# Reordering the first projections of an encoder block: high-part products first, a second load queue, the norm's row first, weight conversions later

## The chip, the cores and the metric

The kernel runs on one core of one Trainium2 chip. The metric is the device time of one execution, in microseconds (us). The times of before are the median and the ends of three runs. The profile is of one further execution, and it has a time of its own.

## The reference

One encoder block on 1024 tokens of width 1024, to which 16 meta tokens are added (1040 in all), in float32:

```python
h = concatenate([meta, x])
proj = rms_norm(h, norm_mix) @ w_in          # 4352 columns: qa ka va qb kb vb and two gates
y_a = differential_attention(qa, ka, va)     # 4 heads, all keys
y_b = windowed_gqa(qb, kb, vb, sink)         # 8 heads on 2 key heads, window 128 and the meta tokens
h = h + (sigmoid(ga) * (y_a @ w_ba) + sigmoid(gb) * (y_b @ w_bb)) @ w_o
h = h + (silu(rms_norm(h) @ w_gate) * (rms_norm(h) @ w_up)) @ w_down
out = rms_norm(h, norm_final)[16:]
```

The change lies in the first microseconds: the norm of the first tokens, and the projections to kb and to the first two 128-column parts of qb.

## The kernel before, in words

**Products in three terms.** A float32 operand is held as a high part (rounded to fp32r by ScalarE, line 113 for weights, 146 for tokens) and a low part (what the rounding left, a subtraction at line 114 on POOL or VectorE for weights, 147 on VectorE for tokens). A product is then three matmuls: high by high, high weights by low tokens, low weights by high tokens. `project_steps` (line 201) does a projection of 128 columns: for each chunk of tokens and each of eight 128-row slices c of the weights it issues the three matmuls (line 208) into one PSUM bank, and yields after each slice. When the last slice is done, `evac_split` (lines 221 to 232) takes the bank out, again in a high and a low part, and `kb_consume` or `qb_steps` stores it.

**The first tokens.** Tokens come in tiles of 128. `load_x` (373) loads one, `norm_x` (380) normalises it: ScalarE squares and sums (130), POOL makes the reciprocal root (118, 119), VectorE multiplies by it and by the norm's row `gmix` (136). `turn_x` (387) transposes it on TensorE, four 128x128 blocks to a bank, two banks (144), and takes the banks out into `hT_hi` (146) and `hT_lo` (147). A chunk of kb or qb has 256 tokens, so its matmuls need two tiles turned. `gmix` is loaded as 32 rows and copied twice by VectorE to 128 (409 to 411).

**The weights.** `preload` (172) loads 128 columns of `w_in`; `ensure` (194) loads if needed and converts the next in a fixed order: kb's low part is made on POOL, qb's on VectorE. A third set, `w_q1` (second part of qb), has a tile of its own, shares its buffers with the token tiles, and is split at line 426 with VectorE.

**Keeping TensorE busy.** Fifteen matmuls on zeros (406) at the start and seven more (424), which wait for the first normalised tile, do no part of the result.

**What sets the order.** The kernel's text is written once in program order, but the tile framework schedules this part: it simulates the engines and emits each engine's instructions in the order of that simulation. Each engine then runs its own list in order, waiting at semaphores. DMAs are issued by SP's list, and one DMA waits in that list for all that stand ahead of it. `early` and `advance` (391) interleave the projections with the turning of later tiles. From the differential attention on, the order of the instructions is written out by hand.

The list of SP before begins: token tile 0 (line 376), `gmix` (409), token tile 1, kb's weights, qb's weights (174), `w_q1` (415), token tile 2, two small rows, token tile 3, and so on. Token tile 3 takes the buffer of tile 0, tile 4 that of tile 1, tile 5 that of `w_q1`.

ScalarE's list before: square of tile 0, square of tile 1, kb's conversion, the two takings-out of turned tile 0, qb's conversion, `w_q1`'s conversion, the two takings-out of tile 1, squares of tiles 2 and 3.

VectorE's list before: copies of `gmix`, norm of tile 0, the zeros, norm of tile 1, low parts of tile 0, low parts of qb's weights and of `w_q1`, two small rows (486, 490), low parts of tile 1, norms of tiles 2 and 3.

## Time and profile before

| what | us |
|---|---|
| median of 3 runs | 1447.68 (1447.35 to 1448.65) |
| the profiled execution's own time | 1447.04 |
| its span, first to last instruction | 1445.1 |
| TensorE busy in the span | 1429.7 (99%) |
| VectorE, ScalarE, POOL busy | 901.6, 675.1, 465.3 |

The views give a start in us from the span's start, then the busy time, the engine (PE is TensorE's matmuls, PEld its weight loads, DVE VectorE, ACT ScalarE, SPq and ACTq the DMA-issuing lists of SP and ScalarE), the line in the kernel, the operation, and what it writes and reads. A merged row has a count behind it. Square brackets tell how long the engine was idle ahead of the row and what ended that. The share of TensorE's clock that was granted is the column PEclk.

### The profile page before, as it was taken

To read this page: it belongs to the slowest core of one execution; us is meant where nothing else is said; L and a number is where in the kernel's file an instruction comes from. 1 tells how busy PE (TensorE), PEld (TensorE's weight loads), DVE (VectorE), ACT (ScalarE), POOL (GpSimd) and SP (SyncE) were. 2 spreads that over 40 slices of the span, in tenths; PEclk is the share of its full clock that TensorE was granted. 3 is DMA by queue.
4 is the path that set the end of the run, shared out by engine and by line. 5 is a ranking of instruction groups with operands and counts; after the bars stand their busy time and mean duration, and the time that the engine had idled before them with its cause. 6 is when DMAs were issued, how large, how long until landed. Compare 5 with 4: busy or idle time off the path is not lost.

```text
span 1445.1 us, 20977 instructions
## 1 busy us (share of the span) xinstructions
PE 1429.7 (99%) x7327; PEld 1229.1 (85%) x7327; DVE 901.6 (62%) x1758; ACT 675.1 (47%) x1275; POOL 465.3 (32%) x454
## 2 busy tenths in 40 slices
PE   8999999999999999999999999999999999999998
PEld 6989989888899999888878888888888888888886
DVE  7356426537777778635988875654455443777566
ACT  6355426534554546445345754333333333444444
POOL 4142223322323232221513135454445442000442
PEclk9999999999999999999999999999999999999999
DMA  7334353354424242079341633433223322964343
GB/s 229 87 99 115 108 128 92 89 174 133 139 82 140 89 140 82 22 241 298 117 160 64 191 110 110 146 125 108 97 97 108 102 102 98 342 207 140 125 124 146
DMA packets 159050, 191.67 MB, mean 133 GB/s; under 512 B 16113, under 2 KB 103601, under 8 KB 158945
## 3 DMA queue, kind: packets, MB, share of 16 engines
q1 hardware_dynamic: 158368, 189.28, 41.0%
q8 instruction: 58, 0.95, 0.3%
q10 hardware_dynamic: 576, 1.05, 0.2%
q14 instruction: 48, 0.39, 0.1%
HBM read 129.80 MB, written 53.94 MB: 127 GB/s over the span
## 4 chain that ended last, share of the span: by engine, by line
PE 94%; DVE 2%; DMA 2%; ACT 1%; issue 1%; POOL 0%; SPq 0%; DVEq 0%; ACTq 0%
PE pg L1233 29%; PE pd L1337 14%; PE pp_g L208 12%; PE aps L618 4%; PE po L1137 4%; PE apy L660 3%; PE pp_va L208 3%; PE pp_ka L208 3%; PE pp_qb L208 3%; PE pp_qa L208 3%; PE ppa L562 3%; PE apt L647 2%; PE bpt L346 2%; PE bpy L352 2%; PE bps L321 2%; PE po L1145 2%
## 5 line engine op out<-in xcount | busy, mean ns | idle before, releaser
L1233 PE MATMUL pg<-t,wop 128*128 128x512 f32 x1056 | 242.4, 389 | 0.0
L1233 PEld LDWEIGHTS pg<-t,wop 128*128 128x128 f32 x1056 | 198.3, 188 | 41.1
L1337 PE MATMUL pd<-ob,oa 128*128 128x512 f32 x924 | 209.6, 389 | 0.0
L114 POOL TENSOR_TENSOR wop<-wf,wop 128x512 fp32r<-128x512 f32 x114 | 151.3, 1327 | 164.2 <-ACT wop L113 155.7
L1337 PEld LDWEIGHTS pd<-ob,oa 128*128 128x128 f32 x924 | 173.5, 188 | 36.0
L1233 PE MATMUL pg<-b,wop 128*128 128x512 f32 x792 | 183.3, 390 | 0.4 <-ACT c L1245 0.4
L1233 PEld LDWEIGHTS pg<-b,wop 128*128 128x128 f32 x792 | 148.5, 188 | 31.3 <-ACT c L1245 0.7
L114 POOL TENSOR_TENSOR wl_c<-w_c,wh_c 128x1024 fp32r<-128x1024 f32 x32 | 78.2, 2443 | 154.3 <-ACT wh_c L113 132.6
L113 ACT ACTIVATE wop<-wf 128x512 fp32r<-128x512 f32 x128 | 80.8, 633 | 72.4 <-PE pg L1233 50.8
L629 ACT ACTIVATE as<-as,amn 128x1040 f32<-128x1040 f32 x64 | 74.5, 1165 | 73.6 <-DVE amn L624 73.6
L208 PE MATMUL pp_g<-hT_hi,wh_c 128*128 128x512 f32 x256 | 101.3, 396 | 0.0
L208 PE MATMUL pp_g<-hT_hi,wl_c 128*128 128x512 f32 x256 | 100.9, 394 | 0.0
L208 PE MATMUL pp_g<-hT_lo,wh_c 128*128 128x512 f32 x256 | 100.9, 394 | 0.0
L113 ACT ACTIVATE oa<-ra 128x512 fp32r<-128x512 f32 x77 | 48.7, 632 | 107.9 <-PE pd L1337 48.7
L618 PE MATMUL aps<-ak,aq 128*128 128x352 f32 (+1 forms) x384 | 92.6, 326 | 0.0
L114 POOL TENSOR_TENSOR oa<-ra,oa 128x512 fp32r<-128x512 f32 x27 | 34.9, 1294 | 168.6 <-ACT oa L113 167.2
L1011 DVE TENSOR_TENSOR s<-wf,wf 128x512 f32<-128x512 f32 x22 | 15.9, 724 | 110.0 <-DMA wf<-in_w_ff_up_dram 68.9
L618 PEld LDWEIGHTS aps<-ak,aq 128*128 128x128 f32 x384 | 69.6, 188 | 14.0
L624 DVE CUSTOM_DVE_ANT_0 as<-aps,dist,amn 128x352 f32<-128x352 f32 (+1 forms) x128 | 71.3, 563 | 10.4 <-PE aps L618 8.4
L333 POOL TENSOR_SCALAR bs<-bs,bdn 128x432 f32<-128x432 f32 (+1 forms) x64 | 37.0, 596 | 97.5 <-DVE bdn L331 56.2
L323 DVE CUSTOM_DVE_ANT_0 bs<-bps,tbx,nsink 128x432 f32<-128x432 f32 (+1 forms) x64 | 38.4, 624 | 41.1 <-PE bps L321 38.5
L624 DVE CUSTOM_DVE_ANT_0 as<-aps,dist,far_a 128x352 f32<-128x352 f32 x64 | 37.1, 580 | 43.0 <-PE aps L618 42.8
(276 smaller groups left out, 3049.7 us busy)
## 6 DMA issues: line engine op xcount, KB each, us to landing
ra<-aop SPq DMA_DIRECT2D x77, 256.0 KB, 2.6
w_c<-in_w_in_dram SPq DMA_DIRECT2D x33, 512.0 KB, 3.9
wf<-in_w_ff_gate_dram SPq DMA_DIRECT2D x25, 512.0 KB, 3.6
wf<-in_w_ff_up_dram SPq DMA_DIRECT2D x25, 512.0 KB, 3.6
aop<-as SPq DMA_DIRECT2D x44, 256.0 KB, 2.1
aop<-c SPq DMA_DIRECT2D x33, 256.0 KB, 2.0
g_d<-gate_stage SPq DMA_DIRECT2D x32, 256.0 KB, 2.0
gt<-g_d SPq DMA_DIRECT2D x32, 256.0 KB, 4.3
```

The lines of the kernel that those rows point to most:

```text
L113: nc.scalar.activation(hi, src, AF.Copy)
L114: lo_eng.tensor_tensor(lo, src, f32(hi), ALU.subtract)
L208: nc.tensor.matmul(ps[:, :n], a[:, c, :], b[:, c, at:at + n], start=(c == 0 and i == 0), stop=(c == DC - 1 and i == 2))
L323: nc.vector.tensor_tensor_reduce(st[:, r, :W], ps[:, :W], tb, 2.0 ** -(4 * g + r + 1), nsink[:, 4 * g + r:4 * g + r + 1], ALU.add, ALU.min ...
L562: nc.tensor.matmul(ps, w[:, a, j, :], src(j, b, tk), start=(j == 0 and n == 0), stop=(j == 3 and n == 2))
L618: nc.tensor.matmul(ps[:, :n], qs[m][:, t * P:(t + 1) * P], ks[m][:, vv, k0:k0 + n], start=(vv == 0), stop=(vv == 1))
L624: nc.vector.tensor_tensor_reduce(s[m][:, a:b], ps[:, a - k0:b - k0], far_by, slope, low, ALU.add, ALU.min, mn[:, m, i + j:i + j + 1])
L629: nc.scalar.activation(s[m][:, 0:L], s[m][:, 0:L], AF.Exp, bias=low, scale=-1.0, accum_out=dn[:, m:m + 1])
L660: nc.tensor.matmul(py[:, cols], v[:kp, a, k, :], at_[:kp, k, b, :], start=(k == 0 and j == 0), stop=(k == 8))
L1137: nc.tensor.matmul(sets_o[p][u], oa[:, a, u * P:(u + 1) * P], ob[:, b, :], start=(p in (1, 5) and j == 0 and k == 0), stop=(p in (2, 3) an ...
L1233: nc.tensor.matmul(ps, op[:, x, c, :], b[:, y, c, :], start=(p in (1, 5) and c == 0 and n == 0), stop=(p in (4, 2, 3) and c == 3 and n == ...
L1337: nc.tensor.matmul(ps[u], oa[:, a, u * P:(u + 1) * P], ob[:, b, :], start=(p in (1, 2, 5) and j == 0 and k == 0), stop=(p in (2, 3, 4) and ...
```

## The change

Five edits, all within the first stage:

1. **High parts first.** `project_steps` takes `hi_first`. With it, the first chunk (`at == 0`) issues its eight high-by-high matmuls first and then the sixteen others. It is set for kb and for the first two parts of qb. The number of matmuls and of yields is the same.
2. **Second tokens by ScalarE's queue.** Token tile 1 is issued from ScalarE's list (its first instruction, ahead of the load of the activation table) and no longer from SP's.
3. **The norm's row first.** `gmix` is now SP's first DMA, token tile 0 its second.
4. **Weights' conversions behind the tokens'.** The weights are loaded where they were, but kb's conversion is held back until the last high part of tile 0 is issued, and qb's and `w_q1`'s until that of tile 1 (`tc.issue_after`). The load of token tile 3 moves ahead of `w_q1`'s split in the program's text.
5. **Small rows later.** `gsub` and `nsink` (486, 490) wait for the last low part of token tile 3.

```diff
     def transposed(pp, xn, parts, hi, lo, at, name):
...
-            nc.scalar.activation(h, pt[:, :, :parts], AF.Copy)
-            nc.vector.tensor_tensor(lo[:, 4 * b:4 * b + 4, at:at + parts], pt[:, :, :parts], f32(h), ALU.subtract)
+            high = nc.scalar.activation(h, pt[:, :, :parts], AF.Copy)
+            low = nc.vector.tensor_tensor(lo[:, 4 * b:4 * b + 4, at:at + parts], pt[:, :, :parts], f32(h), ALU.subtract)
+        return high, low
...
-    def project_steps(col, chunks, name, evac):
+    def project_steps(col, chunks, name, evac, hi_first=False):
...
+            turns = [(c, i) for c in range(DC) for i in range(3)]
+            if hi_first and at == 0:
+                turns.sort(key=lambda ci: ci[1] > 0)
+            for u, (c, i) in enumerate(turns):
+                a, b = terms[i]
+                nc.tensor.matmul(ps[:, :n], a[:, c, :], b[:, c, at:at + n], start=(u == 0), stop=(u == 3 * DC - 1))
...
-    load_x(0)
     nc.sync.dma_start(gmix[0:32], norm_mix.broadcast_to([32, D]))
     nc.vector.tensor_copy(gmix[32:64], gmix[0:32])
     nc.vector.tensor_copy(gmix[64:P], gmix[0:64])
-    load_x(1)
-    ensure(2)
+    load_x(0)
+    load_x(1, nc.scalar)
+    preload(C_KB)
+    preload(C_QB)
...
-    turn_x(0)
+    high, _ = turn_x(0)
...
+    with tc.issue_after(high.ins):
+        ensure(1)
+    load_x(3)
+    high, _ = turn_x(1)
     q1_h, q1_l = (bpool.tile([P, DC, P], F32R, tag=tag, name=f"{tag}_q1", bufs=1) for tag in ("wh", "wl"))
-    split(q1_h, q1_l, w_q1, nc.vector)
+    with tc.issue_after(high.ins):
+        ensure(2)
+        split(q1_h, q1_l, w_q1, nc.vector)
     prepped[C_QB + P] = q1_h, q1_l
-    load_x(3)
     norm_x(2)
-    turn_x(1)
-    p_kb = project_steps(C_KB, KB_CHUNKS, "kb", evac_split(None, kb_consume))
+    p_kb = project_steps(C_KB, KB_CHUNKS, "kb", evac_split(None, kb_consume), hi_first=True)
...
-    nc.vector.tensor_scalar(gsub, gsub, 1.0 - LAMBDA_INIT, None, ALU.mult)
+    with tc.issue_after(low.ins):
+        nc.vector.tensor_scalar(gsub, gsub, 1.0 - LAMBDA_INIT, None, ALU.mult)
...
-    nc.vector.tensor_scalar(nsink, sinkb, -1.0, None, ALU.mult)
+    with tc.issue_after(low.ins):
+        nc.vector.tensor_scalar(nsink, sinkb, -1.0, None, ALU.mult)
```

What the scheduler makes of it: ScalarE's list now begins with the DMA of token tile 1, then squares of tiles 0 and 1, the two takings-out of tile 0, kb's conversion, the two of tile 1, qb's and `w_q1`'s conversions, squares of tiles 2, 3 and 4. VectorE's has the low parts of both tiles 0 and 1 ahead of those of qb's weights and `w_q1`. On TensorE the first products are eight high-by-high of kb, one with kb's low tokens, six high-by-high of qb, and only then those with kb's low weights; the whole first chunk (72 matmuls) stands nearly complete ahead of the turning of tiles 2, 3 and 4, which before were mixed into it. Up to the second group's projections of the windowed attention (about 180 us in the profile) the lists differ in places; then they are the same. The counts of all engines' instructions are the same, but for the one DMA that moved.

More of the change, by code (lines that the diff above doesn't have):

```diff
@@ L205, in project_steps @@
             ps = pp_bank(f"pp_{name}_{at}")
-            for c in range(DC):
-                for i, (a, b) in enumerate(terms):
-                    nc.tensor.matmul(ps[:, :n], a[:, c, :], b[:, c, at:at + n],
-                                     start=(c == 0 and i == 0), stop=(c == DC - 1 and i == 2))
-                if c == DC - 1:
+            turns = [(c, i) for c in range(DC) for i in range(3)]
[4 more added lines that the diff above has]
+                nc.tensor.matmul(ps[:, :n], a[:, c, :], b[:, c, at:at + n], start=(u == 0), stop=(u == 3 * DC - 1))
+                if u == 3 * DC - 1:
                     evac(ps[:, :n], at, n)
-                yield
+                if u % 3 == 2:
+                    yield
     def project(col, chunks, name, evac):
@@ L296, in consume @@
                                       st[64 * par:64 * par + 64, hl, :n])
-        return project_steps(C_QB + j * P, QB_CHUNKS if j < 2 else Q_CHUNKS, f"qb{j}", evac_split(qbs[:, j:j + 1], consume))
+        return project_steps(C_QB + j * P, QB_CHUNKS if j < 2 else Q_CHUNKS, f"qb{j}", evac_split(qbs[:, j:j + 1], consume),
+                             hi_first=j < 2)
     def project_qb(g, qb):
@@ L371, in encoder_block, with load_x @@
     xts, xns, done, early = {}, {}, [], []
-    def load_x(t):
+    def load_x(t, queue=nc.sync):
         xts[t] = bpool.tile([P, D], F32, tag="btr", name=f"x_{t}", bufs=4)
         if t < NT:
-            nc.sync.dma_start(xts[t], x[t * P:(t + 1) * P, :])
+            queue.dma_start(xts[t], x[t * P:(t + 1) * P, :])
         else:
@@ L388, in turn_x @@
         parts = P if t < NT else NM
-        transposed(lambda name: bank(psum1, ("bt", "bs")[t % 2], name, 2), xns.pop(t), parts, hT_hi, hT_lo, t * P, f"a{t}")
+        return transposed(lambda name: bank(psum1, ("bt", "bs")[t % 2], name, 2), xns.pop(t), parts, hT_hi, hT_lo, t * P, f"a{t}")
     def advance(n):
@@ L440, in encoder_block @@
     norm_x(4)
-    turn_x(3)
+    _, low = turn_x(3)
     early += [(p_kb, DC), (p_q0, DC), (p_q1, DC)]
```

## The prediction

> **What bounds the kernel now.** The page comes first, then the waits of TensorE (PE), then the first 25 us of the timeline.

> ```profile
> span 1445.1 us, 20977 instructions
> PE 1429.7 (99%) x7327; PEld 1229.1 (85%) x7327; DVE 901.6 (62%) x1758; ACT 675.1 (47%) x1275; POOL 465.3 (32%) x454
> ```

> ```profile
> PE pp_kb L208 <- DVE hT_lo L147: 2.1, 1, 2.1
> PE ptn_a L144 <- DVE xn_a L136: 1.7, 1, 1.7
> PE pp_kb L208 <- ACT hT_hi L146: 1.4, 1, 1.4
> PE idle L406 <- DVE zeros L403: 1.2, 1, 1.2
> PE po L1137 <- DVE gt L912: 1.1, 1, 1.1
> PE bps L321 <- DVE bmn L323: 1.0, 3, 0.4
> ```

> PE is the bound. Of its longest waits (total, count, longest in us) four lie in the first 16.5 us; the next is 1.1. So whatever brings PE's real work forward in the first stage should come out at the end one for one, and nothing else in this change can matter much. The profiled execution took 1447.04, 1.94 over its span, and lies 0.64 under the median of the three runs (1447.68).

> ```profile
> 0.72 0.40 SPq L376 DMA_DIRECT2D x<-in_x_dram  x1
> 1.17 0.42 SPq L409 DMA_DIRECT2D gmix<-in_norm_mix_dram  x1
> 1.17 5.99 PE L406 MATMUL idle<-zeros 128*128 128x512 bf16 x15 [1.17 <-DVE zeros L403]
> 4.95 1.06 ACT L130 ACTIVATE xn_a<-x 128x1024 f32<-128x1024 f32 x1 [2.95 <-DMA x<-in_x_dram]
> ...
> 7.49 1.28 DVE L136 SCALAR_TENSOR_TENSOR xn_a<-x,rstd_a,gmix 128x1024 f32<-128x1024 f32 x1 [0.72 <-POOL rstd_a L119]
> 7.63 1.06 ACT L130 ACTIVATE xn_a<-x 128x1024 f32<-128x1024 f32 x1 [1.53 <-DMA x<-in_x_dram]
> ...
> 8.83 1.09 PE L144 MATMUL ptn_a<-ident,xn_a 128*128 128x128 f32 x8 [1.67 <-DVE xn_a L136]
> ...
> 9.76 1.67 PE L424 MATMUL idle<-zeros 128*128 128x512 bf16 x7
> ...
> 10.26 3.22 POOL L114 TENSOR_TENSOR wl_c<-w_c,wh_c 128x1024 fp32r<-128x1024 f32 x1 [0.33 <-ACT wh_c L113]
> ...
> 12.20 1.06 ACT L113 ACTIVATE wh_q<-w_q 128x1024 fp32r<-128x1024 f32 x1
> 12.36 2.20 DVE L114 TENSOR_TENSOR wl_c<-w_c,wh_c 128x1024 fp32r<-128x1024 f32 x1
> 13.16 1.06 ACT L146 ACTIVATE hT_hi<-ptn_a 128x512 fp32r<-128x512 f32 x2
> 13.79 0.39 PE L208 MATMUL pp_kb<-hT_hi,wh_c 128*128 128x256 f32 x1 [1.41 <-ACT hT_hi L146]
> 14.14 0.28 PE L208 MATMUL pp_qb<-hT_hi,wh_q 128*128 128x256 f32 x1
> 14.48 1.21 DVE L114 TENSOR_TENSOR wl_q<-w_q,wh_q 128x1024 fp32r<-128x1024 f32 x1
> 15.75 1.28 DVE L147 TENSOR_TENSOR hT_lo<-ptn_a,hT_hi 128x512 fp32r<-128x512 f32 x2
> 16.48 0.44 PE L208 MATMUL pp_kb<-hT_lo,wh_c 128*128 128x256 f32 x1 [2.06 <-DVE hT_lo L147]
> 19.92 0.36 PE L208 MATMUL pp_qb<-hT_hi,wl_c 128*128 128x256 f32 x1
> ```

> The first product starts at 13.79. After three of them PE stops until 16.48, because VectorE (DVE) splits the weights of qb and `w_q1` (2.20 and 1.21) ahead of the low part of token tile 1. From 16.48 to 19.92 sixteen products start, 0.215 each. The rate afterwards is in one row of the chain (start, us, count): 0.118 each.

> ```profile
> 29.04 1.89 PE pp_kb L208 x16
> ```

> The windows of the span say why (stretch, length, busy time of PE, PEld, DVE, ACT and POOL, then the granted clock, the DMA share and GB/s):

> ```profile
> 16.00:17.00 1.00, 0.52 (x3) 0.52 (x4) 1.00 (x3) 0.40 (x2) 0.80 (x3) 0.83 0.88 266
> 17.00:18.00 1.00, 1.00 (x7) 1.00 (x6) 1.00 (x2) 0.00 (x0) 0.32 (x1) 0.50 0.85 280
> 20.00:22.00 2.00, 2.00 (x18) 2.00 (x18) 1.28 (x1) 0.00 (x0) 0.49 (x1) 0.98 1.11 411
> ```

> The clock halves at about 16.66 and returns at about 20.08, 3.4 us later. I measure the stage by an **effective start**: when the first chunk's 72 products would have to start to run without a gap at 0.118. Before, 19 products had started by 19.92: 19.92 - 19 x 0.118 = **17.7**.

> **The change part by part.**

> *Second queue and norm's row.* These decide the sum. Tile 0 is issued at 0.72 and landed by 4.95, when its square starts. The view of transfers gives the two behind it, from issue to landing:

> ```profile
> x<-in_x_dram SPq DMA_DIRECT2D x1, 512.0 KB, 6.0
> gmix<-in_norm_mix_dram SPq DMA_DIRECT2D x1, 128.0 KB, 4.2
> ```

> Tile 1 needs 6.0 (landed 7.63), behind all that was queued ahead. `gmix` (1.17 + 4.2 = 5.4) was not late: tile 0's norm waited for POOL until 7.49. Putting it first removes no wait and moves tile 0's issue 0.45 back. And tile 1, issued on ScalarE's list at the same moment, no longer waits behind tile 0. No row of the start has two queues loading; the end of the kernel has, when SP (q1) and ScalarE (q10) store together:

> ```profile
> q10 hardware_dynamic: 93, 0.19, 50.2%
> q1 hardware_dynamic: 95, 0.19, 49.8%
> ```

> Equal halves. So tile 0 (with `gmix` ahead, 640 KB) and tile 1 (512 KB) finish near together, near where tile 1 landed. Bounds for tile 0's landing: 5.4 (4.95 + 0.45, no sharing) and 7.63 (tile 1's row). I take 6.9, nearer the upper, a little under it because `gmix`'s two small shares now fall into the slow first microseconds. [...]

> From tile 0's landing to its transposes: 8.83 - 4.95 = 3.88, unchanged (square, POOL, norm). They start at 10.8, not 8.83. Tile 1's own norm is no longer late: its square follows tile 0's at once.

> *The clock.* PE's first idle products end at 7.16, so the gap is 3.6 us, not 1.67. A gap of 2.06 (with 0.6 of work and 1.41 of idling ahead of it) halved the clock, the 1.67 did not. I take it as halved at 10.8 and back 3.4 us of work later, at 14.2.

> *Stage by stage.* Eight transposes at half rate (twice 0.11 each): 12.6. Seven idle products: four at 0.40 (5.99 / 15, the half rate) until 14.2, three at 0.24 (1.67 / 7): 14.9. Tile 1's first four transposes, 0.55: 15.45; ScalarE's first taking-out, 0.53: 16.0, the second 16.55. Then eight high-by-high products of kb and one low: 9 x 0.118, 17.05. qb's conversion now stands behind both takings-out: 16.55 + 1.06 = 17.6; six high-by-high of qb, 18.3. kb's low weights: tile 0 taken out at 13.15, conversion 14.2, POOL 3.22, 17.45, in time. Fifteen products by 18.3 is an effective start of 18.3 - 15 x 0.118 = **16.55**, a gain of **1.15 us**.

> *High parts first* adds no matmul. It gives PE 14 products to do while POOL and DVE make low parts, which is what covers the 2.06 gap. *Conversions later* takes 3.4 us of DVE from ahead of `hT_lo` of tile 1, and two of ScalarE's 1.06 from ahead of its `hT_hi`. The price is that low weights are late next: qb's would be ready at 19.8 (17.6 + 2.20), and PE needs them after kb's other 15 products and eight more, at 21.0 (18.3 + 23 x 0.118). *Small rows later* frees at most 0.1 us of DVE (between the end of `w_q1`'s split, 15.69, and the low part's start, 15.75): nothing, as `hT_lo` is no longer last.

> *What is late behind it.* SP's list is in order; token tile 5 takes `w_q1`'s buffer, which is free only when DVE has split it (15.7 before, now about 19.9), and tile 3 waits for tile 0's norm (2 us later). Tile 5's square stands on ScalarE between the takings-out of tiles 2 and 3.

> ```profile
> 23.51 2.53 DVE L147 TENSOR_TENSOR hT_lo<-ptn_a,hT_hi 128x512 fp32r<-128x512 f32 x4 [0.35 <-ACT hT_hi L146]
> ```

> Before, tile 3's low part was done at 26.04 and its first use was at 29.04: 3 us of cover. Now the use comes at 16.55 + 72 x 0.118 + 24 transposes (2.7) = 27.75, and DVE gets there at 27.5 to 29; half of it is enough for the first 12 products. I cost it at nothing; without that cover it is up to 1 us. The mixed order of the windowed attention is worth between +1.0 and -1.0 (PE's only waits there, L321, are 1.0 in three); I take 0.

> Sum: 1447.04 - 1.15 = 1445.9, and for the median of runs 0.64 more: **1446.5**.

> **The rivals.**

> 1. *The clock holds across the 3.6 us gap.* Then transposes 10.8 to 11.7, idle products to 13.4, `hT_hi` of tile 1 at 14.4 and 14.95, qb's conversion 16.0, its six products 16.7; POOL's low weights 16.6. Effective start 16.7 - 1.77 = 14.95: 2.75 gained, 1444.9. For it: the 1.67 gap did no harm. Against: the 2.06 gap did. [...]
> 2. *No sharing at the start: tile 0 lands at 5.4.* Its transposes start at 9.3, the gap is 2.1, the clock holds. Idle products to 11.9, `hT_hi` of tile 1 at 12.9 and 13.45, conversion 14.5, six products 15.2: effective start 13.45, gain 4.25, 1443.4. Against: the equal halves of the tail.
> 3. *Slower: the half clock lasts through the stage.* Tile 0 lands at 7.63, transposes 11.5 to 13.25, seven idle products at 0.40 to 16.05, `hT_hi` of tile 1 at 17.5 and 18.0, conversion 19.1, six products at half rate 20.4: effective start 18.6, a loss of 0.9, 1448.6. It decides from the point where the clock returns after about 16.
> 4. *Tile 5 comes late and takes the gain.* Issued at 20, landing after up to 6.0 (tile 1's row), its square, from 26.0 and not from 25, holds up tile 3's taking-out and PE's second chunk by 0.9: gain 0.25, 1447.4. For it: the buffer is 4 us later. Against: less is queued ahead of it, so 4 is likelier.

> **How the numbers follow.** Forecast 0.45, rival 1 0.17, rival 2 0.12, rival 3 0.12, rival 4 0.14. 0.2% is 2.9 us (about what a measurement of this kernel can tell from no change), so "faster" is below 1444.8 and "slower" above 1450.6. Below lie rival 2 (0.12), nearly half of rival 1 (0.07) and the forecast's edge (0.05): 0.24. Above is only rival 3 with a second bad step: 0.04. Within: 0.72. The range takes in the forecast, rivals 1, 3 and 4, and rival 2 almost to its value: 1443.6 to 1448.8.

> **What would show it.** Right: ScalarE's first square starts at 6.5 to 7.5, PE's first transposes near 10.8, a PEclk under 1 somewhere between 9 and 15 and none at 16 to 20, the first product near 16.0, and after it no PE wait over 0.6 in the stage. A first square at 5.4 is rival 2; a first square at 7 with fast transposes is rival 1; a first product after 17 is rival 3; a PE wait near 28 is rival 4. What would make all of it wrong is a PE wait after 60 us that before did not have.

## The result and the profile after

| | before | after |
|---|---|---|
| median of the runs side by side, us | 1448.24 (1446.22 to 1451.5, 22 runs) | 1446.41 (1443.65 to 1448.74, 22 runs) |
| the profiled execution's own time | 1447.04 | 1446.66 |
| its span | 1445.1 | 1444.8 |

The ratio is 0.9985, with a 95% interval from 0.9979 to 0.9992: 1.83 us less, faster by less than the 0.2% that the prediction took as its bound. The forecast was 1446.5.

The page of after, its first rows:

```profile
span 1444.8 us, 20969 instructions
PE 1429.3 (99%) x7327; PEld 1227.7 (85%) x7327; DVE 904.0 (63%) x1758; ACT 674.4 (47%) x1275; POOL 470.2 (33%) x454
```

TensorE's waits in after (total, count, longest, in us):

```profile
PE ptn_a L145 <- DVE xn_a L136: 4.1, 1, 4.1
PE idle L413 <- DVE zeros L410: 1.2, 1, 1.2
PE po L1152 <- DVE gt L927: 1.2, 1, 1.2
PE apt L662 <- DVE as L650: 1.0, 1, 1.0
PE pg L1248 <- ACT c L1260: 0.9, 1, 0.9
PE bps L328 <- DVE bmn L330: 0.3, 1, 0.3
PE pp_kb L214 <- ACT hT_hi L147: 0.3, 1, 0.3
```

The waits of 2.1 and 1.4 ahead of kb's first products have shrunk to one of 0.3. In their place the wait for the first normalised tile is 4.1, not 1.7. The timeline of after, first 18 us (start, length, engine and line; the line numbers are those of the changed kernel, up to 15 above those of before):

```profile
6.75 1.06 ACT L130 ACTIVATE xn_a<-x 128x1024 f32<-128x1024 f32 x1 [4.30 <-DMA x<-in_x_dram]
7.80 1.04 ACT L130 ACTIVATE xn_a<-x 128x1024 f32<-128x1024 f32 x1
8.86 1.28 DVE L136 SCALAR_TENSOR_TENSOR xn_a<-x,rstd_a,gmix 128x1024 f32<-128x1024 f32 x1 [2.93 <-POOL rstd_a L119]
10.19 1.13 PE L145 MATMUL ptn_a<-ident,xn_a 128*128 128x128 f32 x8 [4.09 <-DVE xn_a L136]
11.05 1.28 DVE L136 SCALAR_TENSOR_TENSOR xn_a<-x,rstd_a,gmix 128x1024 f32<-128x1024 f32 x1 [0.45 <-POOL rstd_a L119]
11.12 3.19 PE L432 MATMUL idle<-zeros 128*128 128x512 bf16 x7
12.99 2.35 POOL L114 TENSOR_TENSOR wl_c<-w_c,wh_c 128x1024 fp32r<-128x1024 f32 x1 [1.98 <-ACT wh_c L113]
14.11 1.25 PE L145 MATMUL ptn_a<-ident,xn_a 128*128 128x128 f32 x8
15.58 1.29 DVE L148 TENSOR_TENSOR hT_lo<-ptn_a,hT_hi 128x512 fp32r<-128x512 f32 x2 [2.05 <-ACT hT_hi L147]
15.61 1.23 PE L214 MATMUL pp_kb<-hT_hi,wh_c 128*128 128x256 f32 x8 [0.25 <-ACT hT_hi L147]
17.85 0.28 PE L214 MATMUL pp_kb<-hT_hi,wl_c 128*128 128x256 f32 x1
```

Tile 0 is 1.80 later (6.75 against 4.95), its transposes 1.36, the first product 1.82 (15.61 against 13.79), but from there on nothing stops: fifteen products stand ahead of 17.85, so the effective start is 17.85 - 15 x 0.118 = 16.08, against 17.7. The windows of after (granted clock third from the end):

```profile
10.00:11.00 1.00, 0.81 (x7) 0.81 (x8) 0.56 (x2) 0.11 (x1) 0.92 (x2) 1.00 1.17 383
11.00:12.00 1.00, 1.00 (x6) 0.43 (x5) 0.95 (x1) 1.00 (x3) 0.01 (x1) 0.56 1.07 335
14.00:15.00 1.00, 1.00 (x8) 0.89 (x7) 0.00 (x0) 0.04 (x1) 1.00 (x1) 0.74 0.29 77
17.00:18.00 1.00, 0.95 (x8) 0.96 (x9) 0.97 (x1) 1.00 (x2) 0.00 (x0) 1.00 0.66 187
```

The 3.41 us of half clock that lay on the products from 16.66 now lies from 11.1 to 14.5 on the idle products and the first transposes of tile 1. How far the first stage as a whole has moved can be read from the first product of vb, behind kb and qb. The view of that tile, in before and then in after (count, ns least/median/most, first start to last):

```profile
L208 PE MATMUL pp_vb<-hT_hi,wh_c x24: 286/335/341, 58.2 to 69.8; 128*128 128x384 f32 x16, 128*128 128x272 f32 x8
```

```profile
L214 PE MATMUL pp_vb<-hT_hi,wh_c x24: 286/335/341, 56.9 to 68.5; 128*128 128x384 f32 x16, 128*128 128x272 f32 x8
```

The stage is **1.3 us** ahead. When the same matmul is compared by its number in the two traces, the lead is 1.32 at 57 us and 1.9 from 180 to 336 us: the waits of the windowed attention (L321, three with 1.0 in all; now L328, one of 0.3) give 0.6 more. Then this execution gives back 1.2 around `apt` (a wait of 1.0) and 0.5 at `pg` (0.9 against 0.4 in before). These two belong to the single execution: the changed kernel's second trace (below) has no `apt` wait and 0.5 at `pg`, and ends 1.93 ahead. So the medians' 1.83 agrees with the lead of 1.9, and the 0.38 between the two profiled executions does not contradict it.

### The profile page after: what moved, and what is told of

Read it like the earlier page. It is cut to its first block, busy times and chain, and to the rows that moved or that the text cites. A ratio compares the mean times of both kernels' runs of the same rounds, so it can differ in the third digit from the quotient of the medians.

```text
span 1444.8 us, 20969 instructions
## 1 busy us (share of the span) xinstructions
PE 1429.3 (99%) x7327; PEld 1227.7 (85%) x7327; DVE 904.0 (63%) x1758; ACT 674.4 (47%) x1275; POOL 470.2 (33%) x454
## 4 chain that ended last, share of the span: by engine, by line
PE 94%; DVE 3%; DMA 1%; ACT 1%; issue 1%; POOL 0%; SPq 0%; DVEq 0%; ACTq 0%
PE pg L1248 29%; PE pd L1352 14%; PE pp_g L214 12%; PE aps L633 4%; PE po L1152 4%; PE apy L675 3%; PE pp_va L214 3%; PE pp_ka L214 3%; PE pp_qb L214 3%; PE pp_qa L214 3%; PE ppa L577 3%; PE apt L662 2%; PE bpt L353 2%; PE bpy L359 2%; PE bps L328 2%; PE po L1160 2%
## 5 line engine op out<-in xcount | busy, mean ns | idle before, releaser
L114 POOL TENSOR_TENSOR wop<-wf,wop 128x512 fp32r<-128x512 f32 x114 | 154.2, 1354 | 162.5 <-ACT wop L113 150.7
L114 POOL TENSOR_TENSOR wl_c<-w_c,wh_c 128x1024 fp32r<-128x1024 f32 x32 | 77.3, 2416 | 170.2 <-ACT wh_c L113 160.0
L113 ACT ACTIVATE wop<-wf 128x512 fp32r<-128x512 f32 x128 | 80.7, 632 | 74.3 <-PE pg L1248 44.9
L113 ACT ACTIVATE oa<-ra 128x512 fp32r<-128x512 f32 x77 | 48.7, 632 | 108.3 <-PE pd L1352 50.1
L114 POOL TENSOR_TENSOR oa<-ra,oa 128x512 fp32r<-128x512 f32 x27 | 35.0, 1296 | 168.6 <-ACT oa L113 167.2
L1026 DVE TENSOR_TENSOR s<-wf,wf 128x512 f32<-128x512 f32 x22 | 15.2, 692 | 113.0 <-DMA wf<-in_w_ff_up_dram 61.5
L113 ACT ACTIVATE wh_c<-w_c 128x1024 fp32r<-128x1024 f32 x33 | 34.9, 1059 | 63.7 <-PE pp_g L214 28.1
L340 POOL TENSOR_SCALAR bs<-bs,bdn 128x432 f32<-128x432 f32 (+1 forms) x64 | 37.1, 599 | 82.3 <-DVE bdn L338 57.6
## 6 DMA issues: line engine op xcount, KB each, us to landing
w_c<-in_w_in_dram SPq DMA_DIRECT2D x33, 512.0 KB, 4.1
wf<-in_w_ff_gate_dram SPq DMA_DIRECT2D x25, 512.0 KB, 3.8
wf<-in_w_ff_up_dram SPq DMA_DIRECT2D x25, 512.0 KB, 3.8
```

What stands on the lines that cost most here:

```text
L113: nc.scalar.activation(hi, src, AF.Copy)
L114: lo_eng.tensor_tensor(lo, src, f32(hi), ALU.subtract)
```

## The experiments

**The theories.** The prediction's, A: loading tile 1 beside tile 0 delays tile 0, that halves the clock early, and the order of products together with the late conversions earns more than this costs. Against it: B1, the start is not what matters, since token tile 5, whose buffer comes free late, takes any gain; B2, the halved clock decides; B3, the order of products or the late conversions are worth nothing by themselves.

In the expectations of the single runs "theory A" and "theory B" are what stands there. Ratios are to before on the same chip, whose medians were 1447.77 (33 runs, first group), 1447.89 (30, second) and 1447.44 (26, third); after was measured beside 1448.24, as above. The ratios differ by up to 0.0006 from the quotients of the medians, so the two columns can put close kernels in a different order. "Square", "turn" and "product" are the starts of tile 0's square, of its transposes and of the first product; "vb" is the first product of vb (the stage's end), all in the one profiled execution. A lead is the time by which TensorE is ahead of before at the same number of matmuls; the time given with it is that of before up to 33 us.

| kernel | median | ratio, 95% interval | square | turn | product | vb |
|---|---|---|---|---|---|---|
| before | | 1 | 4.95 | 8.83 | 13.79 | 58.2 |
| after | 1446.41 | 0.9985 [0.9979, 0.9992] | 6.75 | 10.19 | 15.61 | 56.9 |
| again (1st) | 1446.08 | 0.9988 [0.9978, 0.9998] | 6.52 | 9.97 | 15.25 | 56.5 |
| x1_sp (1st) | 1444.88 | 0.9986 [0.9976, 0.9995] | 4.80 | 8.25 | 11.98 | 57.6 |
| x0_first (1st) | 1445.05 | 0.9983 [0.9975, 0.9992] | 5.10 | 9.03 | 12.95 | 59.1 |
| long_idle (1st) | 1446.34 | 0.9994 [0.9985, 1.0003] | 6.31 | 9.76 | 13.48 | 56.7 |
| tile5_early (2nd) | 1443.98 | 0.9971 [0.9960, 0.9982] | 4.87 | 8.32 | 12.05 | 53.5 |
| x0_tile5 (2nd) | 1444.88 | 0.9976 [0.9967, 0.9984] | 5.09 | 8.99 | 12.72 | 55.4 |
| conv_early (2nd) | 1445.54 | 0.9987 [0.9977, 0.9996] | 6.74 | 10.20 | 15.82 | 56.4 |
| no_hi (2nd) | 1447.4 | 0.9994 [0.9985, 1.0003] | 6.52 | 9.97 | 13.70 | 55.4 |
| queue_only (3rd) | 1449.6 | 1.0016 [1.0007, 1.0025] | 6.83 | 10.27 | 16.70 | 60.4 |
| after_t5 (3rd) | 1446.17 | 0.9988 [0.9980, 0.9997] | 6.57 | 10.02 | 16.52 | 58.0 |
| t5_again (3rd) | 1442.74 | 0.9970 [0.9958, 0.9981] | 5.45 | 8.89 | 12.62 | 53.9 |
| t5_no_hi (3rd) | 1443.36 | 0.9971 [0.9960, 0.9982] | 5.17 | 8.62 | 12.35 | 54.1 |

### again: the changed kernel once more

No edit.

> The changed kernel, unchanged. In the profile after, PE's work was 1.3 us ahead of before when the stage ended (57 us) and 1.9 ahead at 180 us, then lost 1.2 at a wait of 1.0 for VectorE near 340 us (L662) and 0.5 near 840 us. Theory (the waits belong to that one execution): neither wait comes back, and the median is 1.5 to 2 us under before. Rival (they belong to the changed order): the same two waits come back at the same places, and each costs 0.5 to 1.2 us in every run.

Tile 0's square is at 6.52, the gap ahead of the transposes 2.85, the half clock from 9.77 to 13.19, the stage 1.7 ahead (56.5 against 58.2). The windows of again, which show both ends of the half clock:

```profile
8.00:10.00 2.00, 0.03 (x1) 0.03 (x1) 1.33 (x2) 0.71 (x2) 1.73 (x2) 0.94 1.16 353
12.00:14.00 2.00, 2.00 (x8) 0.81 (x7) 1.31 (x3) 1.52 (x2) 0.40 (x1) 0.70 0.65 232
```

The late tile and an early half clock are in both traces; the wait at `apt` is not in this one, and that at `pg` is 0.5. Two traces of one kernel differ by 0.4 at the stage's end, so differences below that mean nothing in the table, and where the clock differs between two traces even larger ones can be the execution's.

### x1_sp: tile 1 back on SP's queue

```diff
-    load_x(1, nc.scalar)
+    load_x(1)
```

> One part undone: token tile 1 goes by SP's queue again, behind the norm's row and tile 0. All engines' orders stay the same but for that DMA. Theory (the second queue takes half of the transfers from tile 0): tile 0 lands at 5.4 and not at 6.7, ScalarE's first square starts at 5.4, the transposes at 9.3, the gap on PE shrinks from 4.1 to 2 to 3 us; effective start 13.5 (clock holds) to 15 (it halves), against 16.1 after: 1.1 to 2.6 us faster than the changed kernel. Rival (tile 0 is late because it stands behind the norm's row, in the slow first microseconds): its square stays at 6.5 or later and the time stays within 0.5 us of the changed kernel.

The timeline of x1_sp:

```profile
4.80 1.06 ACT L130 ACTIVATE xn_a<-x 128x1024 f32<-128x1024 f32 x1 [2.80 <-DMA x<-in_x_dram]
6.94 1.06 ACT L130 ACTIVATE xn_a<-x 128x1024 f32<-128x1024 f32 x1 [0.99 <-DMA x<-in_x_dram]
8.25 1.09 PE L145 MATMUL ptn_a<-ident,xn_a 128*128 128x128 f32 x8 [2.31 <-DVE xn_a L136]
24.52 1.06 ACT L130 ACTIVATE xn_a<-x 128x1024 f32<-128x1024 f32 x1 [2.80 <-DMA x<-in_x_dram]
25.58 1.07 ACT L147 ACTIVATE hT_hi<-ptn_a 128x512 fp32r<-128x512 f32 x2
26.21 0.39 PE L214 MATMUL pp_kb<-hT_hi,wh_c 128*128 128x256 f32 x1 [2.13 <-ACT hT_hi L147]
```

Tile 0 comes 1.95 earlier than in after, tile 1 (6.94 against 5.4 in after) later: the second queue shares the transfers, and the later of the two tiles has landed by 6.75 with it and by 6.94 without. That part of A is shown. TensorE is 5.2 ahead at 27 us. Then tile 5's square (24.52) waits 2.80 for its load, tile 3's taking-out stands behind it on ScalarE, and TensorE stops 2.13; the clock is halved from 27.8 to 31.3, and of the lead 0.5 is left at 33 us. So B1 holds in this trace, and the gain of an early tile 0 is paid away. The profiled run lies 1.4 over this kernel's median, so not every execution loses as much; the ratio, 0.9986, is that of after, and the 1.1 to 2.6 us expected on top of after (1.2 by the medians of this kernel and again) are not shown. The views of transfers issued from 13 to 20 us (count, KB, median us to landing), of x1_sp and then of tile5_early below:

```profile
w_c<-in_w_in_dram SPq DMA_DIRECT2D x2, 512.0 KB, 6.1
x<-in_x_dram SPq DMA_DIRECT2D x2, 512.0 KB, 8.2
```

```profile
x<-in_x_dram SPq DMA_DIRECT2D x2, 512.0 KB, 3.8
w_c<-in_w_in_dram SPq DMA_DIRECT2D x2, 512.0 KB, 6.6
```

### x0_first: tile 0 ahead of the norm's row, tile 1 on SP's queue

```diff
+    load_x(0)
     nc.sync.dma_start(gmix[0:32], norm_mix.broadcast_to([32, D]))
...
-    load_x(0)
-    load_x(1, nc.scalar)
+    load_x(1)
```

> Two parts undone: SP's queue has tile 0, the norm's row, tile 1, as before; high parts first and the later conversions stay. Theory: tile 0 lands at 4.95, PE's transposes start at 8.83, the clock holds over a gap of 1.7 or less, tile 1's transposes at 11.3 to 11.5, first product 12.5 to 12.9, effective start 13.0: 4.7 us under before and 3 us under the changed kernel. Rival A (the norm's row is what tile 0 waits for): the norm of tile 0 starts no earlier than in the changed kernel. Rival B (tile 1, which lands at 7.6 again, is what the first product waits for): first product 14 or later and less than 1.5 us under the changed kernel.

The same picture: 4.2 ahead at 26 us, then tile 5's square at 25.98 after a wait of 3.24, a TensorE wait of 2.2, half clock from 28.76 to 32.17, and in this execution 0.9 behind before at the stage's end (vb at 59.1). That execution took 1447.9, 2.85 over the kernel's median of 1445.05. What its rows show is one of the ways it can go, and not the usual one.

### long_idle: no gap ahead of the transposes

```diff
-    for _ in range(15):
+    for _ in range(28):
...
-    norm_x(2)
+    with tc.issue_after(high.ins):
+        norm_x(2)
```

> The changed kernel with 28 products on zeros at the start in place of 15, so that they end at 8.8 to 10.6 and the gap ahead of the first transposes (at 10.2) is under 1.5 us; token tile 2's norm is tied behind tile 1's taking-out so that the orders stay the same. Theory (the half clock from 11.1 to 14.5 comes from that gap): no half clock there, seven products on zeros in 1.7 and not 3.2 us, effective start 14.4 to 14.7, median 1 to 1.7 us under the changed kernel. Rival (the clock's fall has another cause, or the stage is bound by conversions anyway): the first product stays at 15.4 or later and the time within 0.4 us of the changed kernel.

The gap is 0.7, the clock is never halved, the seven idle products take 1.67 (after: 3.19), and the first product is 2.1 earlier than in after, 0.4 of it because tile 0 itself was earlier (6.31 against 6.75). From the square to the first product it takes 7.2, in after 8.9. So in this execution, without the gap, there is no half clock at the start, and the half clock of after costs about 1.7 us there. At the stage's end only 0.2 is left (56.7 against 56.9): tile 5's square waits 1.90 for its load, TensorE stops 1.23 at 26.82 behind it, and the lead falls from 3.7 at 27 us to 1.4 at 33 us. The ratio, 0.9994 [0.9985, 1.0003], shows no gain. B2 is right that the gap can bring the half clock; what its absence earns goes, in this kernel, to the stop behind tile 5.

### tile5_early: x1_sp, with tile 5 ahead of vb's and qa's weights

```diff
-    load_x(1, nc.scalar)
+    load_x(1)
...
-    load_x(6)
+    last = load_x(6)
+    with tc.issue_after(last.ins):
+        preload(C_VB)
+        preload(C_QA)
```

> Token tile 1 by SP's queue (as x1_sp) and, new, the loads of the weights of vb and qa tied behind that of token tile 6, so that tiles 5 and 6 are ahead of them in SP's queue. In x1_sp tile 5 was issued at 15.8 and its square started at 24.5; the taking-out of tile 3 stands behind that square, PE waited 2.1 us at 26.2 and ran 3.4 us at half clock from 28.7. Theory (tile 5's transfer, behind 1 MB of weights, took x1_sp's gain): its square starts by 22, no PE wait over 0.6 near 26, no half clock near 28.7; at 57 us PE's work is about 5 ahead of before in place of 0.6, and the median is 4.5 to 6 us under before. Rival (VectorE or the evictions hold the second chunk anyway): a PE wait of 1.5 or more stays near 24 to 27 and the time stays within 1 us of x1_sp.

SP's list has tiles 5 and 6 at 15.85 and the weights behind them at 18.28; in x1_sp the weights stood ahead, at 13.47, and the tiles' transfers took 8.2 instead of 3.8 (fences above). Tile 5's square starts at 21.73 without a wait, TensorE doesn't stop, the clock isn't halved, and the stage is 4.7 ahead (53.5). The median is 3.9 under before (4.5 to 6 expected). B1 is shown in the trace: with an early tile 0 the next limit was tile 5's place in the queue. In time the intervals of this kernel and of x1_sp still overlap.

### x0_tile5: the same cure with tile 0 ahead of the norm's row

```diff
+    load_x(0)
     nc.sync.dma_start(gmix[0:32], norm_mix.broadcast_to([32, D]))
...
-    load_x(0)
-    load_x(1, nc.scalar)
+    load_x(1)
...
+    with tc.issue_after(last.ins):
+        preload(C_VB)
+        preload(C_QA)
```

> The same cure on x0_first (tile 0 ahead of the norm's row). x0_first's first product was at 12.95, 0.97 later than x1_sp's in its profile, and its square of tile 5 at 26.0. Theory (the order of tile 0 and the norm's row is worth little; tile 5 took the gain): stage ends 4.3 ahead of before, median 4 to 5 us under before and within 1 us of the kernel with the norm's row first. Rival (the norm's row first is itself a cost of 0.45): 0.4 to 1 us faster than the kernel with the norm's row first.

Tile 0's square is not earlier (5.09; with `gmix` first it stands at 4.87, 5.45 and 5.17), but from the square to the transposes it takes 3.90. So it is in all traces of the table: 3.88 to 3.93 where tile 0 is first (before, x0_first, x0_tile5), 3.44 to 3.46 in the eleven where `gmix` is first. The reason is on POOL. Before, VectorE's second copy of `gmix` and POOL's first operation:

```profile
6.08 0.69 DVE L411 COPY gmix<-gmix 64x1024 f32<-64x1024 f32 x1
6.20 0.62 POOL L118 TENSOR_SCALAR rstd_a<-ss_a 128x1 f32<-128x1 f32 x1 [2.37 <-ACT xn_a L130]
```

and in after:

```profile
5.23 0.69 DVE L417 COPY gmix<-gmix 64x1024 f32<-64x1024 f32 x1
7.99 0.19 POOL L118 TENSOR_SCALAR rstd_a<-ss_a 128x1 f32<-128x1 f32 x1 [4.15 <-ACT xn_a L130]
```

With `gmix` late its copy runs while POOL works on one number per row, which then takes 0.62 and not 0.19 (0.67 and 0.65 in the two others with tile 0 first). Tile 1 too is earlier with `gmix` first (square at 6.46 against 7.60). The medians (1443.98 and 1444.88) belong to ratios with overlapping intervals, so the gain in time is likely and not proved. Both halves of the theory missed in size: the stage is 2.8 ahead and not 4.3, the median 3.0 under before and not 4 to 5; the lead falls from 4.4 at 27 us to 3.4 at 29, and by another 0.4 at a wait at vb's first product.

### conv_early: the conversions not held back

```diff
-    with tc.issue_after(high.ins):
-        ensure(1)
+    ensure(1)
...
-    with tc.issue_after(high.ins):
-        ensure(2)
-        split(q1_h, q1_l, w_q1, nc.vector)
+    ensure(2)
+    split(q1_h, q1_l, w_q1, nc.vector)
```

> The changed kernel with one part undone: the conversions of the weights are no longer held back (ScalarE's list has kb's ahead of tile 0's takings-out, qb's and w_q1's ahead of tile 1's). Theory A (the prediction's step: they stand in the way of hT_lo of tile 1): first products wait for it again, effective start 17 or later, 1 to 2 us slower than the changed kernel. Theory B (with tile 0 landing at 6.7, ScalarE and VectorE are idle 2 us ahead of each tile, and the conversions fit there): no later than the changed kernel, effective start 15.6 to 16.1, time within 0.6 us.

The low parts of tile 1 come 2.2 later than in after (17.81 against 15.58). But the scheduler now puts kb's, qb's and `w_q1`'s 24 high-by-high products first, and TensorE does not stop. The timeline of conv_early:

```profile
15.82 0.74 PE L214 MATMUL pp_kb<-hT_hi,wh_c 128*128 128x256 f32 x4 [0.25 <-ACT hT_hi L147]
17.81 1.28 DVE L148 TENSOR_TENSOR hT_lo<-ptn_a,hT_hi 128x512 fp32r<-128x512 f32 x2
18.76 0.28 PE L214 MATMUL pp_kb<-hT_lo,wh_c 128*128 128x256 f32 x1
```

The stage is 1.8 ahead, against 1.3 and 1.7 in the two traces of the changed kernel. With the order of the products there, holding back the conversions is worth nothing that can be seen. The profiled run itself took 1449.3, 3.8 over this kernel's median: TensorE waited 2.16 at `apt`, and behind that the clock was halved from 341.3 to 344.7.

### no_hi: the old order of the products, conversions held back

```diff
-            if hi_first and at == 0:
+            if False and hi_first and at == 0:
```

> The changed kernel without high parts first (slice by slice, three terms each, as before); the rest of the change stays. Theory A (the prediction's step: the 14 high-by-high products cover the wait for the low parts): a PE wait of about 2 us for hT_lo comes back after the first product, effective start 17.5 to 18. Theory B (with the conversions behind, VectorE makes tile 1's low part 0.6 after its high part, and POOL has kb's low weights by 15.3): a wait of 0.6 at most, effective start 16.1 to 16.3, time within 0.5 us of the changed kernel.

```profile
13.70 0.39 PE L214 MATMUL pp_kb<-hT_hi,wh_c 128*128 128x256 f32 x1 [0.25 <-ACT hT_hi L147]
14.42 0.38 PE L214 MATMUL pp_kb<-hT_lo,wh_c 128*128 128x256 f32 x1 [0.34 <-DVE hT_lo L148]
15.13 0.38 PE L214 MATMUL pp_qb<-hT_hi,wh_c 128*128 128x256 f32 x1 [0.32 <-ACT wh_c L113]
```

No stop of 2 us comes back: the low part of tile 1 follows 0.34 late, the high weights of qb 0.32. In this execution the clock was not halved, though the gap was 3.59, and the stage is 2.8 ahead of before; later it waited 1.5 at `apt` and 1.4 at `pg`. So with the conversions held back the order of the products covers 0.7 of waiting in this trace. The ratio, 0.9994, lies about 1.3 us above that of after and 0.9 above that of again, and its interval overlaps theirs and takes in 1: in time neither theory is shown.

### queue_only: norm's row first and the second queue alone

An edit of before:

```diff
-    load_x(0)
     nc.sync.dma_start(gmix[0:32], norm_mix.broadcast_to([32, D]))
...
-    load_x(1)
+    load_x(0)
+    load_x(1, nc.scalar)
```

> The kernel before with norm's row first and tile 1 on ScalarE's queue alone; conversions, order of the products and small rows as before. Theory A (these two edits alone cost the stage, since tile 0 lands at 6.7 and not by 4.95, and the order of products and conversions pays it back): a PE wait of about 2 us on hT_lo of tile 1 is there again behind the first product (15.5 to 16), effective start 17.7 to 18.5, stage 0 to 0.8 behind before, median 1448 to 1449. Theory B (the late start gives DVE and ScalarE idle time in which the conversions fit, so the order of products and conversions is worth little): first product 15.5 to 16, no wait over 0.6 behind it, stage 1.0 to 1.8 ahead of before, median within 0.7 of the changed kernel's 1446.4.

This is the one kernel that is slower than before: 1.0016 [1.0007, 1.0025], 2.2 us. The timelines of VectorE, POOL and TensorE in queue_only:

```profile
11.06 2.35 POOL L114 TENSOR_TENSOR wl_c<-w_c,wh_c 128x1024 fp32r<-128x1024 f32 x1
11.13 3.37 DVE L136 SCALAR_TENSOR_TENSOR xn_a<-x,rstd_a,gmix 128x1024 f32<-128x1024 f32 x1 [0.45 <-POOL rstd_a L119]
15.62 1.21 DVE L114 TENSOR_TENSOR wl_c<-w_c,wh_c 128x1024 fp32r<-128x1024 f32 x1
16.75 1.21 DVE L114 TENSOR_TENSOR wl_q<-w_q,wh_q 128x1024 fp32r<-128x1024 f32 x1
18.02 1.27 DVE L147 TENSOR_TENSOR hT_lo<-ptn_a,hT_hi 128x512 fp32r<-128x512 f32 x2
18.75 0.39 PE L208 MATMUL pp_kb<-hT_lo,wh_c 128*128 128x256 f32 x1 [1.43 <-DVE hT_lo L147]
```

Tile 0 is late as in after; the conversions of qb and `w_q1` stand ahead of the low part of tile 1, and TensorE stops for 1.43 (2.06 in before). The windows of queue_only:

```profile
14.00:16.00 2.00, 2.00 (x9) 1.36 (x8) 2.00 (x4) 0.77 (x1) 0.00 (x0) 0.54 0.26 53
16.00:17.00 1.00, 0.75 (x7) 0.51 (x5) 1.00 (x2) 0.94 (x2) 0.00 (x0) 1.00 0.86 311
20.00:21.00 1.00, 1.00 (x7) 1.00 (x6) 0.49 (x1) 0.24 (x2) 0.92 (x2) 0.50 1.15 347
```

The clock is halved twice: from 9.00 to 15.82, and behind the stop of 1.43 again from 19.24 to 22.65. The stage ends 2.2 behind before. A is shown, and by more than it expected (0 to 0.8 behind, 1448 to 1449 us): these two edits alone lose, and the order of the products and the late conversions win it back and more. The trace to compare with is after_t5's below, which has the same first half clock and ends the stage 0.2 to 0.4 ahead (the small rows, which the two edits alone leave where they were, take 0.13 of VectorE ahead of the low part). With conv_early and no_hi beside it, the traces show B3 in a way that neither theory had: **either one of the two is enough to remove the long stop; with neither, it comes back.** In time this is shown for conv_early (0.9987 [0.9977, 0.9996]) and not for no_hi.

### after_t5: the changed kernel, with tile 5 ahead of vb's and qa's weights

```diff
+    last = load_x(6)
+    with tc.issue_after(last.ins):
+        preload(C_VB)
+        preload(C_QA)
```

> The changed kernel with the loads of the weights of vb and qa tied behind tile 6's load; tile 1 stays on ScalarE's queue. Theory A (in the changed kernel tile 5 is covered: its square showed no wait at 25.28): the stage stays 1.3 to 1.7 ahead of before, median within 0.6 of 1446.3. Theory B (tile 5 holds it back there too): stage over 2 ahead, median below 1445.5.

The median is after's. In this execution the half clock lasted two stretches of 3.41, from 8.97 to 15.80, and the lead at the stage's end is 0.2 to 0.4 and not 1.3; so A's first half (the stage) missed, most likely for that reason; its second held. With a late tile 0, tile 5 is not the limit.

### t5_again and t5_no_hi: the fastest kernel once more, and without the order of products

```diff
-            if hi_first and at == 0:
+            if False and hi_first and at == 0:
```

> The fastest kernel so far once more (tile 1 on SP's queue, loads of vb's and qa's weights behind tile 6's), unchanged, as the yardstick of the next one on the same chip. If its gain is real: stage 4.5 to 5.2 ahead of before, median 3 to 4.5 below before's. If it was a lucky small sample (6 runs): less than 2.5 below.

> The kernel of t5_again with the first chunk's products in their old order (the order of high parts first is switched off). Theory A (high parts first covers the making of the low parts once tile 0 is early): PE waits on hT_lo or on low weights of 1 to 2 us in all return before 20 us, stage 3 to 4 ahead of before, median 1 to 2 above t5_again. Theory B (with the conversions held back the low parts are in time anyway): PE waits under 0.7 in all before 20 us, stage within 0.7 of t5_again's, median within 0.7 of it.

t5_again is tile5_early unchanged: 1442.74, 0.9970 [0.9958, 0.9981], the stage 4.3 ahead (4.5 to 5.2 expected), the median 4.7 under before (3 to 4.5 expected). Both samples have six runs, and their intervals agree: about 0.3% under before, and most likely faster than the changed kernel, whose intervals in after and again overlap theirs by 0.0004 or less. On the same chip, eight of after_t5's eleven runs lie above the slowest of t5_again's six. Without the order of the products (t5_no_hi) TensorE waits 0.34 for the low part and 0.32 for qb's high weights; the lead at the stage's end is 0.2 smaller, though tile 0 was 0.3 earlier, and the medians cannot be told apart. That is B of this pair, as in no_hi.

## Why the prediction was right, and where it was not

**The late tile 0** was right in cause and size: 6.9 forecast, 6.7 measured. The transfers of after, issued in the first 1.6 us:

```profile
x<-in_x_dram ACTq DMA_DIRECT2D x1, 512.0 KB, 4.7
x<-in_x_dram SPq DMA_DIRECT2D x1, 512.0 KB, 5.5
```

Tile 1, issued at 0.72, lands first, at 5.4; tile 0, issued at 1.18, at 6.7. x1_sp, where one queue has both tiles and tile 0's square is at 4.80, shows that the sharing is the reason. (How much it is worth varies: the square comes at 4.80 to 5.45 in the four kernels with the norm's row first and one queue, at 6.31 to 6.83 in the seven with two.)

**"Putting it first removes no wait and moves tile 0's issue 0.45 back"** was the wrong step. Nothing of 0.45 shows at tile 0's square (4.95 to 5.10 with tile 0 first, 4.80 to 5.45 with the norm's row first), and the chain from square to transposes is 0.44 shorter. The transposes came at 10.19 and not at 10.8: 0.2 from the landing, 0.4 from here. The wait for POOL was in a row that the prediction quoted (the norm's 0.72, ended by POOL's L119); it was taken as given, and not asked why POOL's first step ran from 6.20.

**The clock** was right in this execution (halved from 11.1 to 14.5; 10.8 to 14.2 forecast), but the step "a gap of 2.06 halved the clock, the 1.67 did not", read as a limit on the gap's length, does not stand. A gap of 3.59 left the clock whole (no_hi), one of 1.43 among work halved it (queue_only), and 3.3 to 3.5 halved it for 6.8 us (after_t5, queue_only).

What the traces show in its place: in each of the fourteen, the changes of the granted clock lie whole multiples of 3.413 us apart (before: 6.43, 16.67 and 20.08; after: 4.29, 11.11 and 14.53), on a grid whose first change comes anywhere from 3.95 to 6.87 (4.29 and 6.36 in the two traces of the changed kernel). That first change is read from the idle products, which in after start every 0.43 up to 4.14 and every 0.21 from there; PEclk has 1.00 for both. What tells the stretches apart is TensorE's idle time between two marks of that grid. Up to TensorE's last matmul, nine stretches at full clock had 2.00 to 2.85 us of idling, and half clock followed each of them. All others had 1.89 or less, and half clock followed only one (1.68, queue_only from 15.82). At half clock, 1.04 (after_t5) and 1.28 (queue_only) of idling kept it for another stretch. The gap of 2.85 in again fell with 2.65 into one stretch, and the 3.59 of no_hi was cut by a mark into 1.88 and 1.71. The grid also sets the gap: fifteen idle products end at 5.9 (x1_sp, first change at 3.95) to 7.4 (x0_tile5, 6.87), the later the later the clock rises. This is read from the traces, with one exception; no run moved the gap against the grid. Which half clock an execution gets is thus in part chance.

Rival 1 is nearly an execution of the same stage, with the lead of 2.75 that it was given (no_hi: 58.2 - 55.4 = 2.8), and rival 3's half clock is nearly another (after_t5), with a lead of 0.2 to 0.4 and not the loss of 0.9; between them stand after and again with 1.3 and 1.7. The forecast of one half stretch was the middle case, and that the profiled execution had it was partly luck. (The half rate of the idle products was taken as 0.40 (5.99 / 15); the rows have 0.43, since the last of the fifteen ran at full clock; over four products that is 0.1.)

**High parts first and conversions later** were costed as if each earned its own part: 14 products "covers the 2.06 gap", the conversions "takes 3.4 us of DVE from ahead of `hT_lo`". Together they earned what was forecast; in the traces each alone removes nearly all of the stop, and the second one adds little. The 3.4 was itself inflated: the 2.20 of qb's split in before ran beside POOL's split of kb's weights, which lasted until 13.48, and ended 1.08 behind it. In queue_only the same split takes 1.21, about 1 less, and there it is the norm of tile 1 that takes 3.37 and not 1.28, and ends 1.09 behind POOL's 13.41.

**The sum.** The effective start came at 16.08 and not at 16.55, as the transposes were 0.6 earlier; of the 1.6 gained there 1.3 was left at the stage's end (1.7 in the second trace), where 1.15 was forecast: the term of the start was mis-sized by 0.45, most of it by the step on the norm's row. The windowed attention's order, taken as 0 within 1.0 either way, gave 0.6; 0.5 to 0.9 comes between 60 and 180 us in all kernels with the rest of the change, and nothing in queue_only, whose waits at L321 are still 1.0, but which edit does it wasn't tried. 1.3 + 0.6 = 1.9, against 1.83 in the medians. So the gain forecast, 1.15, was 0.7 too small. That the forecast of 1446.5 came within 0.1 of the measured 1446.41 was luck of its anchor: it was built on the median of 1447.68, and before's runs beside after had 1448.24.

**"Whatever brings PE's real work forward in the first stage should come out at the end one for one"** fits several medians (after: 1.9 ahead at 180 us, 1.83 less; queue_only: 2.2 behind, 2.2 more; t5_again: 5.1 ahead, 4.7 less), though not that of no_hi (3.3 ahead, 0.5 less), and it does not hold for one execution: the waits at `apt` (0 to 2.2) and `pg` (0.3 to 1.5) change from trace to trace of kernels that are the same there. The prediction had named a new wait after 60 us as what would make all of it wrong; the 1.0 at `apt` was one, and as again, the same kernel, has none, it belonged to that execution.

**Rival 4, tile 5**, was wrongly put for the changed kernel and right as a mechanism: it takes the gain as soon as the start is earlier (x1_sp, x0_first, long_idle). The reason is not the buffer, as the prediction had it, but the weights ahead in SP's list: in x1_sp and in tile5_early tile 5 is issued at 15.8 alike, and only its transfer differs (8.2 and 3.8).

## What to carry to other kernels

Where the first tile's landing sets the start, don't give another transfer a queue of its own beside it: in this kernel that cost tile 0 about 1.5 us (squares at 6.31 to 6.83 in place of 4.80 to 5.45), and with tile 5 put right the ratio was 0.9988 [0.9980, 0.9997] with the second queue and 0.9970 [0.9958, 0.9981] without it. When an early gain of several us disappears within the stage, look for the next load that the earlier work now waits for, and at what stands ahead of it in its queue. Two edits that cover the same stop must be tried apart and together, as their worths don't add.
